# A channel shuffle on one core: other sizes for the first tiles and for the last

## The chip, the core and the metric

The kernel runs on one core of a Trainium2 chip. The metric is device time in microseconds (us) of one execution. The kernel before took 316.17 us (median of three runs, 316.07 to 316.84).

## What is computed

The input is 16 x 64 x 64 pixels with 256 float32 channels each. The channels form 8 groups of 32. The reference turns the (group, channel in group) order of each pixel into (channel in group, group):

```python
x = x.reshape(batch, h, w, groups, channels_per_group)
x = x.transpose(0, 1, 2, 4, 3)
x = x.reshape(batch, h, w, c)
```

No arithmetic is done. Each of the 65,536 pixels is 1 KB; 67.11 MB are read from HBM and 67.11 MB written.

## The kernel before

A tile has 128 partitions, and each partition holds q consecutive pixels, so q KB. In what follows such a tile, or such a part of one, is called "q KB" after its size in one partition; it moves q x 128 KB in all. One kilobyte in all 128 partitions is called a row here: 131,072 bytes. The whole input is 512 rows.

The list `_SLOTS` (L12) says how the 512 rows are cut. Each inner list is one slot: one input tile and one output tile. Each number in it is a part with transfers and a copy of its own. Before, there are two parts of 4 and 8 KB in the first slot, 28 KB in the second, twelve slots of 38 KB, and a last one of 16 KB. All tiles are allocated at the size of the biggest slot (L46, L47). There are two input buffers (L13) and three output buffers (L14), used in turn.

For each slot the loop at L45 does this:

- L55: SyncE's queue (SPq in the profile) issues one read per part, HBM to the input tile. When the slot is at least the third, the issue waits until VectorE has copied out of the input tile two slots earlier.
- L57: VectorE (DVE) copies each part, once its read has landed, from the input tile to the output tile. The permutation is in the access pattern. When the slot is at least the fourth, the copy waits until the output tile three slots earlier has been written to HBM.
- L61: ScalarE's queue (ACTq) issues the write of each part, once its copy is done.

The order on each engine is the order of the program. Reads and writes are thus two queues of transfers, which the page of the profile calls q1 (reads) and q10 (writes), and both are served by the same 16 DMA engines. A read or write of q KB consists of 128 pieces of q KB, one for each partition, and each of the 16 engines moves 8 of them. Each transfer also takes one of eight semaphores in turn; the issue waits until the transfer that had it before has landed.

Of the kernel before, what the change touches and what calls it, by code (L numbers as in the profile page):

```python
# [1 line left out]

# [4 lines left out]


F32 = mybir.dt.float32
P = 128  # L10

_SLOTS = [[4, 8], [28]] + [[38]] * 12 + [[16]]  # L12
_IN_BUFS = 2  # L13
_OUT_BUFS = 3  # L14


@with_exitstack
def kernel(
    ctx: ExitStack,
    tc: tile.TileContext,  # L20
    x: bass.AP,
    groups: bass.AP,
    out: bass.AP,
):
    nc = tc.nc
    b, h, w, c = x.shape
    G = int(groups)
    CPG = c // G
    assert G * CPG == c
    assert sum(map(sum, _SLOTS)) * P == b * h * w  # L30
    biggest = max(map(sum, _SLOTS))

    x_flat = x.rearrange("b h w c -> (b h w c)")
    out_flat = out.rearrange("b h w c -> (b h w c)")

    in_pool = ctx.enter_context(tc.tile_pool(name="in_pool", bufs=_IN_BUFS))
    out_pool = ctx.enter_context(tc.tile_pool(name="out_pool", bufs=_OUT_BUFS))

    def rows(flat, first, q):

        return flat[first * c : (first + P * q) * c].rearrange("(p f) -> p f", p=P)

    ctx.enter_context(tc.manual_schedule(engines=None))
    first = 0
    for parts in _SLOTS:  # L45
        in_tile = in_pool.tile([P, biggest * c], F32, name="in_tile")  # L46
        out_tile = out_pool.tile([P, biggest * c], F32, name="out_tile")  # L47
        at = 0
        pieces = []
        for q in parts:  # L50
            pieces.append((q, first, slice(at * c, (at + q) * c)))
            first += P * q
            at += q
        for q, start, cols in pieces:
            nc.sync.dma_start(out=in_tile[:, cols], in_=rows(x_flat, start, q))  # L55
        for q, start, cols in pieces:
            nc.vector.tensor_copy(  # L57
                out=out_tile[:, cols].rearrange("p (i j g) -> p i j g", j=CPG, g=G),
                in_=in_tile[:, cols].rearrange("p (i g j) -> p i j g", g=G, j=CPG),
            )  # L60
            nc.scalar.dma_start(  # L61
                out=rows(out_flat, start, q), in_=out_tile[:, cols]
            )


# [1 line left out]
_INS = ['x', 'groups']  # L67
_OUTS = [((16, 64, 64, 256), 'float32')]

_NUMBERS = {'groups': 8}  # L70


# [26 lines left out]
```

## Time and profile before

| what | value |
|---|---|
| median of three runs | 316.17 us (316.07 to 316.84) |
| span of the profiled execution, first to last instruction | 314.4 us |
| median time less that span | 1.8 us |
| VectorE busy | 119.0 us, 38% of the span, 16 copies |
| moved by the DMA engines | 134.22 MB, 427 GB/s over the span |
| transfers | 16 reads and 16 writes |

Only the span of the profiled execution is recorded, not its own device time; the timed runs stand 1.8 us above it by their median, for what lies around the first and the last instruction. The profile's page has a row with the busy share of the 16 DMA engines in 40 equal slices of the span (a 9 is 90% or more) and under it the GB/s. A packet in it is one piece of one partition, counted in the slice in which it starts, so that a slice or window can show a share over 1. The trace also holds the start, duration and size of each packet; where a text here says "packet by packet", it is read from there. Times in it count from the first instruction, as in the page.

### The profile page before, as it was taken

To read this page: it belongs to the slowest core of one execution; us is meant where nothing else is said; L and a number is where in the kernel's file an instruction comes from. 1 tells how busy PE (TensorE), PEld (TensorE's weight loads), DVE (VectorE), ACT (ScalarE), POOL (GpSimd) and SP (SyncE) were. 2 spreads that over 40 slices of the span, in tenths; PEclk is the share of its full clock that TensorE was granted. 3 is DMA by queue.
4 is the path that set the end of the run, shared out by engine and by line. 5 is a ranking of instruction groups with operands and counts; after the bars stand their busy time and mean duration, and the time that the engine had idled before them with its cause. 6 is when DMAs were issued, how large, how long until landed. Compare 5 with 4: busy or idle time off the path is not lost.

```text
span 314.4 us, 132 instructions
## 1 busy us (share of the span) xinstructions
DVE 119.0 (38%) x16; POOL 0.2 (0%) x4
## 2 busy tenths in 40 slices
DVE  2081907309109109019028028037046055065400
POOL 0000000000000000000000000000000000000000
DMA  7999999999999999999999999999999999999997
GB/s 317 405 441 416 435 416 483 401 465 406 450 421 446 426 436 436 401 470 396 475 396 475 396 470 401 470 401 470 401 450 421 446 426 436 436 417 450 429 421 321
DMA packets 4608, 134.22 MB, mean 427 GB/s; under 512 B 512, under 2 KB 512, under 8 KB 768
## 3 DMA queue, kind: packets, MB, share of 16 engines
q1 hardware_dynamic: 2304, 67.11, 49.8%
q10 hardware_dynamic: 2304, 67.11, 49.4%
HBM read 67.11 MB, written 67.11 MB: 427 GB/s over the span
## 4 chain that ended last, share of the span: by engine, by line
DMA 76%; DVE 19%; issue 0%; SPq 0%; DVEq 0%
DMA in_tile<-in_x_dram 76%; DVE out_tile L57 19%; SPq L55 0%; DVEq L57 0%
## 5 line engine op out<-in xcount | busy, mean ns | idle before, releaser
L57 DVE COPY out_tile<-in_tile 128x9728 f32<-128x9728 f32 (+4 forms) x16 | 119.0, 7440 | 179.4 <-DMA in_tile<-in_x_dram 179.4
L80 POOL MEMSET const-uint8-127<- 128x1 uint8 x1 | 0.1, 103 | 0.0
L80 POOL MEMSET const-bfloat16-1.0<- 128x1 bf16 x1 | 0.1, 102 | 0.0
L80 POOL MEMSET const-float32-1.0<- 128x1 f32 x1 | 0.1, 100 | 0.0
L80 POOL MEMSET const-float32-0.0<- 128x1 f32 x1 | 0.1, 99 | 0.2 <-issue 0.2
## 6 DMA issues: line engine op xcount, KB each, us to landing
in_tile<-in_x_dram SPq DMA_DIRECT2D x12, 4864.0 KB, 37.0
out_dram<-out_tile ACTq DMA_DIRECT2D x12, 4864.0 KB, 42.6
in_tile<-in_x_dram SPq DMA_DIRECT2D x1, 3584.0 KB, 14.7
out_dram<-out_tile ACTq DMA_DIRECT2D x1, 3584.0 KB, 30.9
in_tile<-in_x_dram SPq DMA_DIRECT2D x1, 2048.0 KB, 30.4
out_dram<-out_tile ACTq DMA_DIRECT2D x1, 2048.0 KB, 15.2
in_tile<-in_x_dram SPq DMA_DIRECT2D x1, 1024.0 KB, 5.4
out_dram<-out_tile ACTq DMA_DIRECT2D x1, 1024.0 KB, 25.0
```

The costliest lines, as they stand in the source:

```text
L57: nc.vector.tensor_copy(out=out_tile[:, cols].rearrange("p (i j g) -> p i j g", j=CPG, g=G), in_=in_tile[:, cols].rearrange("p (i g j) -> ...
L80: nc = _bacc.Bacc("TRN2", target_bir_lowering=False, num_devices=1)
```

## The change

The list of slots is replaced. The first slot has three parts of 4, 6 and 8 KB, the second two of 12 and 16 KB, the third one of 24 KB. Eleven slots of 38 KB follow, one fewer than before, and the last slot has 24 KB in place of 16 KB. The sum is 512 rows as before. There are 15 slots and 18 reads, copies and writes, where there were 15 slots and 16 of each. Buffers, queues and the loop are the same.

```diff
-_SLOTS = [[4, 8], [28]] + [[38]] * 12 + [[16]]
+_SLOTS = [[4, 6, 8], [12, 16], [24]] + [[38]] * 11 + [[24]]
 _IN_BUFS = 2
 _OUT_BUFS = 3
```

## Prediction

> **What bounds the kernel now.** I read the page's rows of slices first, then the table of queues, then the chain, and last the packets one by one.
>
> ```profile
> DVE  2081907309109109019028028037046055065400
> ...
> DMA  7999999999999999999999999999999999999997
> ...
> DMA packets 4608, 134.22 MB, mean 427 GB/s; under 512 B 512, under 2 KB 512, under 8 KB 768
> ...
> q1 hardware_dynamic: 2304, 67.11, 49.8%
> q10 hardware_dynamic: 2304, 67.11, 49.4%
> ```
>
> The DMA row is full in all slices but the first and the last, and the packets of the two queues fill 49.8 + 49.4 = 99.2% of what 16 engines have in the span. VectorE is idle most of the time. So the 16 DMA engines are the bound, and from the first transfer to the last there is no hole in them. The chain of waits could mislead here:
>
> ```profile
> DMA 76%; DVE 19%; issue 0%; SPq 0%; DVEq 0%
> ```
>
> It gives VectorE 19%, as if a shorter copy would shorten the kernel. But the chain follows one thread of work. While VectorE copies, the engines move other tiles: the window from 100 to 150 us, with three copies in it, has a DMA share of 1.01.
>
> ```profile
> 0.00:5.00 5.00, 0.94 (x1) 0.20 (x4) 1.00 0.64 241
> ...
> 100.00:150.00 50.00, 20.66 (x3) 0.00 (x0) 1.00 1.01 436
> ...
> 310.00:315.00 5.00, 0.00 (x0) 0.00 (x0) 1.00 0.53 226
> ```
>
> Packet by packet, the first read starts at 1.75 us and the last write ends at 313.27. The span is thus 1.75 us ahead of the first packet, 311.5 us in which all engines work, and 1.2 us behind the last.
>
> **What the engines' time consists of.** The median durations of a packet are 159 ns for 4 KB, 309 for 8, 611 for 16, 1062 for 28 and 1439 for 38. From 4 to 38 KB that is (1439 - 159) / 34 = 37.6 ns for each KB, and 159 - 4 x 37.6 = 8.4 ns for each packet whatever its size; each transfer ends with one more packet of 9 ns on each engine. One row costs 8 x 37.6 = 301 ns. The 1024 rows of both directions are 308.3 us, the 32 transfers 32 x (8 x 8.4 + 9) ns = 2.4 us. The packets' durations sum to 312.0 us for each engine. The 1.2 us left over are stalls: packets longer than usual for their size. They are nearly all reads, and all but about 0.01 us of them start before 50 us, in stretches in which all 16 engines read at once: 0.54 us in the first 10 us, 0.24 from 10 to 30, 0.36 from 30 to 40.
>
> **The change, part by part.**
>
> *The bytes*: the same 1024 rows, 308.3 us.
>
> *Two more transfers each way*: 4 x (8 x 8.4 + 9) ns = 4 x 76 = **+0.31 us**. Sizes that the trace lacks (6, 12, 24 KB) lie between sizes that it has, all on one straight line within 1 ns, so I see no room in them.
>
> *The first packet and the end*: the first read is 4 KB, as before, so 1.75 us stays. Behind the last write comes the same run of waits and drains, 1.2 us. 0.
>
> *Issues*: SyncE issues two more reads, in about 0.4 us each (the first three start 0.42 and 0.48 us apart), ahead of their need: five reads, 46 rows or 13.9 us of transfer, are asked for by about 2.9 us. The sixth (24 KB) waits for the 8 KB copy. That read is the third, 18 rows, landed by about 8 us; the copy is 2.0 us, so the issue comes at about 10.5 us, when more than 3 us of reads still stand in the queue, even without any write between them. The first 38 KB read waits for the 16 KB copy in the same manner, with the 24 KB read ahead of it. ScalarE's two more issues are off the path. The semaphores that the issues wait for belong to transfers that landed long before: the 24 KB write waits for the 6 KB write, and so on. 0.
>
> *Copies*: four more small copies and one big one less are a few us on an engine that idles for 179.4 us waiting for reads. What hides them is the reads and writes in the queues. 0, as long as the queues hold something, and that has to be checked at the end of the kernel, since the last copy grows: 3.87 us for 16 KB, and for 24 KB, between the rows 3.87 (4096) and 6.57 (7168), 3.87 + 2048 x 2.70 / 3072 = 5.67.
>
> ```profile
> 294.54 3.87 DVE L57 COPY out_tile<-in_tile 128x4096 f32<-128x4096 f32 x1 [7.62 <-DMA in_tile<-in_x_dram]
> ```
>
> **Will the write queue last through the last copy?** When both queues have work, each engine alternates: one read packet, one write packet, whatever their sizes. Near 10 us the 4 KB writes start 1.27 us apart, one 1.06 us read packet between them. That is why small early writes land late:
>
> ```profile
> out_dram<-out_tile ACTq DMA_DIRECT2D x1, 1024.0 KB, 25.0
> ...
> out_dram<-out_tile ACTq DMA_DIRECT2D x1, 512.0 KB, 14.3
> ```
>
> So in 9 turns (8 packets and the closing one) a small write goes out while a large read comes in, and the reads gain a lead. Before: 22 rows are read when the first write starts (9.12 us); the 4 KB write goes out against 5 packets of 28 KB and 3 of 38 KB, 32 rows, lead 50; the 8 KB write against 38 rows, lead 80; the 28 KB write, 90; then 38 against 38 holds it. At the end the 16 KB read comes in against 38 rows of writes: 68. The trace has (313.27 - 292.61) / 0.301 = 69 rows still to write when the last read ends, so the counting works.
>
> After: the first write is issued at the same 5.2 us. Packets taken ahead of it are now of 8 KB, not 28, so it starts about 6.8 us, with 14 rows read. Then 4 KB against 10 rows (half of the 8 and the 12 KB read), lead 20; 6 against 14, 28; 8 against 20, 40; 12 against 31, 59; 16 against 38, 81; 24 against 38, 95. The last read, 24 against 38, leaves **81 rows**.
>
> Needed are the 24 rows of the last tile itself and what covers its copy: 1.9 us from the last read packet to the copy, as before (292.61 to 294.54), 5.67 for the copy and 1.0 from issue to first packet (0.73 to 1.75 at the start), 8.6 us or 29 rows; 53 in all. 81 less 53 leaves 28 rows, 8.4 us of cover. 0.
>
> *The stalls*: here the trace shows no row for the new order. Nearest below is the kernel from 50 us on, where they are nearly nothing, so -1.2 us; nearest above is the same stretch twice over, since mixed sizes now last longer (the lead takes six writes to settle, not three): +1.2 us. I take 0, since the first 10 us, half of it, are much the same, and what else the reads have alone is spread differently but not longer.
>
> Sum: **+0.3 us**, with -0.9 and +1.5 as ends. On the profiled execution that is 314.4 + 0.3 = 314.7; the median of the runs stands 1.8 above its span, so 316.17 + 0.3 = **316.5 us**. About 0.3%, 0.95 us, is what a measurement of this kernel tells from no change: the line to faster is 315.2, to slower 317.1.
>
> **Rivals.**
>
> *Stalls grow (slower).* Their place is the first 60 us, while reads get more of the engines than writes. For it: 5.7 of the 19 engine-us of stalls fall at 32 to 34 us, when the engines each take two 38 KB reads in a row. Against it: the new sizes rise more gently, so fewer such pairs. Twice the stalls give 316.5 + 1.2 = 317.7; it decides for slower from 0.65 us more than now (0.95 less 0.31).
>
> *Stalls vanish (faster).* 316.5 - 1.2 = 315.3. For it: from 50 us on there are none. Against it: 0.54 us come in the first 10 us, when only reads can run. Even in full this hardly passes the line.
>
> *The write queue runs dry at the end (slower).* It decides if the lead at the last read is under 53 rows. If the lead stayed at the 40 rows of the 8 KB write, 14 fewer at the end, 27 rows would be missing: 27 x 0.301 = 8.1 us, 324.6. That takes engines that share by bytes and not by packets, which the 1.27 us between the small writes and the 69 rows speak against.
>
> *Each further transfer pays a fixed time (slower).* The 512 KB read takes 3.3 us from issue to landing, its packets 1.9 us (1.75 to 3.67); 1.4 us are fixed. If four more transfers paid that unhidden: 5.6 us, 322.1. Against it: 32 transfers would then have left 45 us of holes, and there are 2.9 us outside the packets. The Trainium skill ("DMA: Bandwidth & Descriptors", "Anatomy of one DMA") fits a DMA as about 2.0 us plus its bytes over 436 GB/s, for transfers issued from GpSimd; an estimate by that, four times 2.0 us, would be 8 us more. The trace does not agree for a filled queue: its share is 99.2%.
>
> **How the numbers follow.** The forecast, within 0.3%: 0.68. Stalls grow: 0.14, of which 0.11 pass the line. Stalls vanish: 0.11, of which 0.06 pass it (with the runs' own spread, 0.77 us). Dry queue: 0.04. Fixed time: 0.03. So faster 0.06, same 0.68 + 0.05 + 0.03 = 0.76, slower 0.11 + 0.04 + 0.03 = 0.18. The range takes in the ends of the stalls, 315.3 to 317.7, and leaves out the last two rivals and what passes the ends.
>
> **What would show it.** Right: a DMA row of 9s from the second slice to the last but one, queue shares that sum to about 99%, writes of the first parts that land sooner than 14.3 and 25.0 us, and some 20 us or more from the last copy's start to the end of the span (19.9 before; 81 rows are 24 us of writes from the last read packet, less 1.9, plus 1.2). Wrong: a slice under 9 inside, above all behind the last read; GB/s under 400 over more than one early slice; a copy that waits for a write.

## The result, and the profile after

The changed kernel is slower: 318.4 us as the ratio to the kernel before gives it, 1.0071 with an interval of 1.0049 to 1.0093. The median of its four runs was 318.81 us, beside 316.12 for the kernel before. One of the four took 342.88 us, far from the other three (317.75 to 319.17), and the ratio leaves it out, as the ratios below leave out one run of e1_head (342.25 us) and two of e4_slotwrite (331.15 and 332.01 us). The forecast was 316.5, with 315.3 to 317.7 as its range.

The page of the changed kernel, in the rows that were read before: VectorE and the DMA engines in 40 slices, the GB/s, the packets, the two queues, and the chain.

```profile
DVE  3452528073460550650740830820910901907000
...
DMA  8999999989999999999999999999999999999994
GB/s 308 399 434 473 392 436 418 476 385 432 446 462 403 462 403 462 398 467 398 467 398 467 393 472 403 462 408 457 428 437 428 433 442 422 426 444 433 433 434 214
DMA packets 5184, 134.22 MB, mean 424 GB/s; under 512 B 576, under 2 KB 576, under 8 KB 1088
...
q1 hardware_dynamic: 2592, 67.11, 49.5%
q10 hardware_dynamic: 2592, 67.11, 49.2%
...
another core or an unknown queue 38%; DVE 29%; DMA 23%; SPq 0%; issue 0%; DVEq 0%
```

The ninth slice shows an 8. That is no hole: a packet counts in the slice in which it starts, and by the packets' starts and ends all 16 engines are busy throughout that slice. What differs is the last slice: 4 in place of 7, 214 GB/s in place of 321. Something works there, but not all of it. The end in windows shows it better. The columns are the stretch, its length, VectorE, GpSimd, the granted clock, the mean share of the 16 DMA engines and the GB/s. First the kernel before, then the changed one:

```profile
312.00:313.00 1.00, 0.00 (x0) 0.00 (x0) 1.00 0.65 279
313.00:314.00 1.00, 0.00 (x0) 0.00 (x0) 1.00 0.00 0
```

```profile
312.00:313.00 1.00, 0.00 (x0) 0.00 (x0) 1.00 0.91 393
313.00:314.00 1.00, 0.00 (x0) 0.00 (x0) 1.00 0.12 49
314.00:315.00 1.00, 0.00 (x0) 0.00 (x0) 1.00 0.11 49
```

A share of 0.12 is 2 / 16: two DMA engines work alone for about 2 us while fourteen have finished. The packets say the same. The trace doesn't name the engine of a packet, but each transfer ends with one closing packet on each of the 16 engines, so these 16 times show how far the engines are apart. For the last write, their median is 312.92 us before and 313.13 after, 0.22 later. The latest engine is 0.37 us behind that median before, and 2.21 after; the second latest 1.87. So of the 2.2 us between the two profiled spans (314.44 and 316.66), 0.22 is on all engines, 2.21 - 0.37 = 1.84 is two engines that are late, and 0.17 lies behind the last packet.

The packets also show where the two lose their time. On one engine each packet starts some nanoseconds before the one ahead of it ends, so from 60 us on they can be linked into 16 chains, one for each engine. In the changed kernel 14 packets are over 0.05 us longer than usual for their size. All of them lie on the two chains that end late, 1.94 and 1.87 us in sum, and none on the other fourteen.

The row of the chain (the last one in the first fence above) now puts the most time down to a name that is no engine, and the waits say what VectorE waits for:

```profile
DVE out_tile L57 <- DMA out_dram<-out_tile: 142.6, 11, 14.3
DVE out_tile L57 <- DMA in_tile<-in_x_dram: 28.1, 7, 9.4
```

Before, all 179.4 us of its waiting was for reads. Now eleven copies wait until an output tile has been written: the reads' lead has grown until all three output tiles are in use. That is the most visible difference between the two profiles, and the experiments had to find out whether it is the one that costs.

### The profile page after: what moved, and what is told of

The parts are those of the page before. It is cut to its first block, busy times and chain, and to the rows that moved or that the text cites. A ratio compares the mean times of both kernels' runs of the same rounds, so it can differ in the third digit from the quotient of the medians.

```text
span 316.7 us, 143 instructions
## 1 busy us (share of the span) xinstructions
DVE 120.6 (38%) x18; POOL 0.2 (0%) x4
## 4 chain that ended last, share of the span: by engine, by line
another core or an unknown queue 38%; DVE 29%; DMA 23%; SPq 0%; issue 0%; DVEq 0%
DVE out_tile L57 29%; DMA out_dram<-out_tile 15%; DMA in_tile<-in_x_dram 8%; SPq L55 0%; DVEq L57 0%
## 5 line engine op out<-in xcount | busy, mean ns | idle before, releaser
L57 DVE COPY out_tile<-in_tile 128x9728 f32<-128x9728 f32 (+6 forms) x18 | 120.6, 6698 | 170.7 <-DMA out_dram<-out_tile 142.6
```

Of the source, the lines that this page charges most:

```text
L57: nc.vector.tensor_copy(out=out_tile[:, cols].rearrange("p (i j g) -> p i j g", j=CPG, g=G), in_=in_tile[:, cols].rearrange("p (i g j) -> ...
```

## Which part of the change, and which wait

Three readings were open: A, the waiting for output tiles costs; B, the bigger last tile does; C, the many mixed sizes do by themselves.

**The new head alone (e1_head).** The third slot has 32 KB, so that the sum stays 512 rows with the old end.

```diff
-_SLOTS = [[4, 8], [28]] + [[38]] * 12 + [[16]]
+_SLOTS = [[4, 6, 8], [12, 16], [32]] + [[38]] * 11 + [[16]]
```

> The new head with the old end: slots of 4+6+8, 12+16, 32, eleven of 38 and 16 KB, 18 transfers each way less none, so the two further ones of the changed kernel are in it. The changed kernel is 2.2 us above the one before (ratio 1.0071); in its trace two of the 16 DMA engines end 2 us after the other fourteen, and from the sixth 38 KB copy on the copies wait for output tiles to be written. Theory A (the reads' lead over the writes grows to the three output tiles, and in that state single engines fall behind): the lead comes from the head, so 318 us or more, two or more engines late, copies that wait for writes. Rival B (the bigger last tile leaves engines unevenly finished): 316.5 us, engines within 0.5 us of each other. Rival C (many mixed sizes throw engines out of step, whatever the lead): 318 us or more as with A.

Measured: 1.0146 times the kernel before (1.0124 to 1.0169). Copies wait 144.5 us for output tiles. In its profile four engines end 1.60 to 3.18 us behind the median:

```profile
313.00:314.00 1.00, 0.00 (x0) 0.00 (x0) 1.00 0.27 115
314.00:315.00 1.00, 0.00 (x0) 0.00 (x0) 1.00 0.15 66
315.00:316.00 1.00, 0.00 (x0) 0.00 (x0) 1.00 0.08 33
```

The shares fall step by step as one engine after the other finishes: about 4 of 16, then 2, then 1. The new head alone thus brings a loss, twice that of the changed kernel.

**The new end alone (e2_tail).** Here the second slot has 20 KB in place of 28, for the same reason.

```diff
+_SLOTS = [[4, 8], [20]] + [[38]] * 12 + [[24]]
```

> The old head, with 20 in place of 28 KB, and the new end: slots of 4+8, 20, twelve of 38 and 24 KB; 16 transfers each way. Theory A: the lead is settled by the 4 and 8 KB writes as before, a little higher for the 20 KB write (18 against 10 rows), about 98 rows, so it stays under the 114 of three output tiles: 316.2 us, within 0.5 us, copies that wait for reads. Rival B (the end): 318 us or more with engines late by 2 us. Rival C (mixed sizes at the head): 316.2 us.

Measured: 1.0008 (0.9999 to 1.0017). B falls: with 24 KB at the end the time is the same within 0.17%, 0.5 us, as the prediction's cover for the last copy said.

**The kernel before, with 4+4+4 KB first (e3_pinned).**

```diff
+_SLOTS = [[4, 4, 4], [28]] + [[38]] * 12 + [[16]]
```

> The kernel before with its first slot cut in 4+4+4 KB in place of 4+8, nothing else: one more transfer each way, 0.15 us. The third 4 KB write goes out against 38 KB reads, so by the counting of turns the lead rises by some 30 rows, from 90 to over 114, and copies have to wait for output tiles. Theory A: about 318 us, one or more engines 1 us or more late, copies that wait for writes. Rivals B and C (the end is the old one, and the sizes at the head are fewer than in the changed kernel): 316.3 us, within 0.5 us.

Measured: 1.0075 (1.0062 to 1.0088), copies waiting 152.3 us for output tiles, two engines 2.55 and 2.69 us late. So one small part more is enough for the whole loss, which speaks against C, and A looked right.

**The changed kernel with one write for each slot (e4_slotwrite).** The reads and copies are those of the changed kernel; the first three writes have 18, 28 and 24 KB.

```diff
+        nc.scalar.dma_start(
+            out=rows(out_flat, first, total), in_=out_tile[:, : total * c]
+        )
```

> The changed kernel's slots and reads, with one write for each slot (18, 28, 24 KB, then 38) in place of one for each part; 18 reads, 15 writes. Writes of 18 and 28 KB hold the lead down: by the counting of turns it settles near 80 to 95 rows, under three output tiles. Theory A: 316.3 us, within 0.5 us, engines together at the end, copies that wait for reads. Rival B (the end): 318 us or more. Rival C (mixed sizes): 318 us, or something between, since the read sizes are the changed kernel's.

Measured: 1.0026 (1.0016 to 1.0035), 0.8 us, copies that wait for reads, engines within 0.7 us of each other at the end. Again as A says. But A had so far been tested only by kernels whose small first parts changed too.

**The kernel before with two output buffers (e5_before_two_out).** This makes copies wait for output tiles and changes nothing else. The closing packets gave a second theory beside A, D: some engines fall out of step. In the changed kernel two engines, and in e1_head four, close the third write (8 KB) 1.0 to 1.3 us ahead of the median and stay apart from then on; in the kernel before none does.

```diff
-_OUT_BUFS = 3
+_OUT_BUFS = 2
```

> The kernel before with two output buffers in place of three, nothing else. Its lead of about 90 rows then stands over the 76 rows of two output tiles, so copies wait for output tiles, with the old sizes at the head. The runs so far leave two theories. A (waiting for output tiles is what costs): 318 us or more. D (the first writes come in while the engines move small read packets; some engines take their first write one turn ahead of the others or behind them, stay out of step, and meet longer packets): in the kernel before all 16 engines take the first write in the same turn, so 316.3 us within 0.5 us, and the engines end within 0.5 us of each other although copies wait for writes.

Measured: 1.0000 (0.9990 to 1.0011). Its waits and its DMA row:

```profile
DVE out_tile L57 <- DMA out_dram<-out_tile: 168.1, 13, 14.2
DVE out_tile L57 <- DMA in_tile<-in_x_dram: 13.2, 3, 7.6
```

```profile
DMA  8999999999999999999999999999999999999997
```

VectorE waits even longer for writes here than in the changed kernel, and it costs nothing: the DMA row is full in every slice inside. **A falls**, as far as it is the waiting. All 16 engines are in step (within 0.42 us at the last closing packet). The reads' lead itself is not tested by this run: by the closing packets 64 rows are left to write when the reads end, as in the kernel before, where the changed kernel has 110.

**32 KB slots, with four and with three output buffers (e6_32_four_out, e7_32_three_out).**

```diff
+_SLOTS = [[4, 6, 8], [12, 16], [24]] + [[32]] * 13 + [[26]]
+_OUT_BUFS = 4
```

> The changed kernel's head (4+6+8, 12+16, 24), then thirteen slots of 32 KB and 26 KB last, with four output buffers of 32 KB (128 rows): 20 transfers each way, 0.3 us more than the changed kernel's 18 in packets and closing packets. By the counting of turns from a first write at 9.4 us the lead settles near 108 rows, under four output tiles, so copies wait for reads. A: 316.9 us, within 0.5 us. D: engines out of step as in the changed kernel, 318 us or more, whatever the output buffers.

> The same sizes with three output buffers (96 rows): copies wait for output tiles. A: 318.5 us or more, and more than with four. D: the same time as with four output buffers, 318 us or more.

Measured: 1.0102 (1.0077 to 1.0127) with four buffers, where all copies wait for reads, and 1.0063 (1.0043 to 1.0083) with three, where copies wait 146.1 us for writes. It is slower either way. More telling are the single runs. With four buffers they lie between 316.30 and 321.02 us, with three between 316.33 and 318.71. The profiled run of each is its fastest, and in both no engine is out of step. A fixed cost of these sizes, C, cannot give that: the same program runs at the kernel before's time in one run and 2 to 5 us slower in the next.

## When an engine out of step costs

**No small head at all (e8_plain).**

```diff
+_SLOTS = [[38]] * 13 + [[18]]
```

> No small head at all: thirteen slots of 38 KB and one of 18, 14 transfers each way, two fewer than the kernel before: -0.3 us of packets. The first write comes at about 23 us, while the engines move 38 KB packets; two reads of 38 rows, 23 us of transfer, stand ahead of the third, which waits for the first copy, so the read queue just lasts. A and D both: engines in step, lead about 76 rows, copies that wait for reads: 315.9 us, with more read stalls in the first 23 us (all engines read alone) up to 317. If the DMA row shows a hole near 23 us, the read queue ran dry.

Measured: 1.0498 (1.0478 to 1.0519). Both theories missed. The read queue does run dry near 25 us, 0.6 us of all engines; reads and writes then start together, and the read packets of that moment take 0.5 to 2.0 us longer, 1.4 us of all engines. The rest is a standing loss, seen in the two queues, which before had almost equal shares:

```profile
q10 hardware_dynamic: 2016, 67.11, 50.8%
q1 hardware_dynamic: 2016, 67.11, 47.9%
```

Two engines are out of step, ahead of the other fourteen by 1.2 us more with each tile. This time the two keep nearly all their packets at 1.44 us, and it is the writes of the fourteen that are long: 1.60 us in the mean from 60 to 245 us. Eight packets of 0.16 us more make 1.3 us a tile. So here the long packets lie on the majority, and the two that are out of step have almost none.

**28 KB as one part, in the changed kernel (e9_28), and cut in the kernel before (e10_cut28).**

```diff
+_SLOTS = [[4, 6, 8], [28], [24]] + [[38]] * 11 + [[24]]
```

```diff
+_SLOTS = [[4, 8], [12, 16]] + [[38]] * 12 + [[16]]
```

> The changed kernel with 28 KB as one part in place of 12+16 in its second slot, nothing else: 17 transfers each way. The first write, issued at 5.2 us and started near 9.4, then comes in while the engines move 28 KB read packets of 1.06 us, several times the 0.3 to 0.6 us by which the engines are apart, in place of 12 KB ones of 0.46 us. Theory D: all 16 engines take it in the same turn, stay in step, 316.4 us within 0.5 us, in most runs, although the lead stands at three output tiles and the other mixed sizes are there. Rival C (the mix of sizes, 4, 6, 8, 24 and 24, or the further transfers): 317.5 us or more.

> The kernel before with 12+16 KB in its second slot in place of 28, nothing else: 17 transfers each way, +0.15 us. The first write now comes in among 12 KB packets. Theory D: some engines take it a turn apart, 317.3 us or more in most runs, times that spread over 1 us or more, and the engines out of step at the end by 1 us or more where the profiled run is one of those. Rival C: two sizes more and one transfer more: 316.3 us, within 0.5 us.

Measured: 1.0016 (1.0008 to 1.0025) and 1.0015 (1.0007 to 1.0024). The first time is what D expected, but not for D's reason: three engines are out of step in that profile. Nor is the lead at three output tiles, as was expected: all its copies wait for reads. The second is a miss: two engines are out of step, as expected, and the median run costs 0.34 us, 0.15 of it for one more transfer each way. So being out of step is not yet the cause.

**12 KB as one first part (e11_one_head).**

```diff
+_SLOTS = [[12], [28]] + [[38]] * 12 + [[16]]
```

> The kernel before with 12 KB as one part in place of 4+8 in its first slot: 15 transfers each way, -0.15 us. The first write is issued near 9 us and starts near 13, among 28 KB packets, or at their end among 38 KB ones. Theory D: in step, 316.0 us within 0.4 us. Rival C: the same. It is the candidate to beat the kernel before, by what one transfer less each way is worth; and if engines fall out of step here, small packets are not the only way to it.

Measured: 1.0025 (1.0014 to 1.0036), slower, a miss too. Reads are stalled for 0.73 us, taken over all engines, between 10 and 15 us, when the first write comes in; the kernel before has 0.06 there.

**The changed kernel once more (e12_after_again).**

> The changed kernel once more, beside these. Theory D: whether and how many engines fall out of step is not the same in each run, so 316.4 us in a run in which none does, 317.5 to 319.5 in the others, a spread over 1 us, where the kernel before spreads by some tenths. Rival C (a fixed cost of the sizes): all runs within 0.5 us of each other, near 318.4.

Measured: 1.0054 (1.0031 to 1.0077), twelve runs from 316.50 to 320.96 us, four of them at 316.50 to 316.57. The spread is what D said. (It is not the changed kernel's alone: the kernel before took 317.41 us in one of its runs, e5_before_two_out 317.69, and e10_cut28 317.99.) The profiled run is the one of 316.50, and four engines are out of step in it, more than in the first profile. Its end:

```profile
312.00:313.00 1.00, 0.00 (x0) 0.00 (x0) 1.00 0.91 393
313.00:314.00 1.00, 0.00 (x0) 0.00 (x0) 1.00 0.01 0
```

All 16 engines finish together, so **D falls as it stood**. What differs is by how much they are out of step. By 100 us the four are 1.37 to 1.45 us behind in reads and 1.34 to 1.42 ahead in writes: about one packet of 38 KB, 1.44 us. Their reads lie on the others' writes, edge on edge, and from 100 to 260 us no packet is longer for it. At the end of the reads the lag turns back into nothing, since each engine has the same bytes to move. In the first profile the two were 1.83 and 2.13 us behind. Their packets lay across the others' turns, and one write or read a tile took 0.1 to 0.45 us longer (1.57 to 1.88 us in place of 1.44), at about 102, 125, 149 and 172 us. They dropped back until they were 3.3 and 3.6 us behind in reads, somewhat over one whole turn of a read and a write (2.88 us).

**Further profiles (s1_after, s2_after, s4_head, s6_32_four_out).** The first two are the changed kernel, then the program of e1_head, then that of e6_32_four_out. They were taken to tell two theories apart. S says that an engine out of step costs nothing while its lag is about one packet, and ends late when the lag is larger; its range for one packet of 38 KB, 1.3 to 1.55 us, was drawn from the profiles so far. T says that only the number of such engines counts.

> The changed kernel, for a further profile. S: each engine that is out of step with an offset of 1.3 to 1.55 us near 120 us ends with the others (within 0.5 us); one with 1.57 to 2.9 us ends 1 us or more late, and the time is 316.5 us if there is none of these, 317.5 or more if there is. T: the more engines are out of step, the longer, whatever their offset.

> The changed kernel, for a further profile: as for the one before it.

> The new head with the old end, whose first profile had four engines at offsets of 1.57 to 1.68 us near 105 us, all late at the end by 1.6 to 3.2 us. S: the same where offsets are off 1.3 to 1.55, 316.6 us where they are in it. T: by the number of engines.

> The new head with 32 KB slots and four output buffers, whose profile had no engine out of step (316.3 us) while other runs took 318 to 321 us. One packet of 32 KB is 1.21 us. S: engines out of step at an offset within 0.15 us of 1.21 cost nothing, others end 1 us or more late. T: by the number of engines. With none out of step, 316.3 us, and nothing is told apart.

The table has all profiles with engines of this kind, by the closing packets. The lag in reads is against the median of 16, for the read that closes next after 100 us (for s6_32_four_out the read near 92 us, where a packet has 32 KB and 1.21 us; at its next read, at 111 us, the lag is 1.80); lateness is that at the last write.

| run | us | engines out of step: lag in reads, us | late at the end, us |
|---|---|---|---|
| e12_after_again | 316.50 | 1.37, 1.38, 1.42, 1.45 | none over 0.3 |
| s1_after | 316.39 | 1.37 | none over 0.3 |
| e9_28 | 316.43 | 1.30, 1.49, 1.54 | none over 0.3 |
| e10_cut28 | 316.48 | 1.26, 1.30 | none over 0.3 |
| the changed kernel | 318.44 | 1.83, 2.13 | 1.87, 2.21 |
| s2_after | 318.36 | 1.66, 1.68, 1.91 | 1.69, 2.13, 2.16 |
| e1_head | 319.37 | 1.57, 1.61, 1.62, 1.68 | 1.60, 1.76, 1.96, 3.18 |
| s4_head | 318.88 | 1.59, 1.64, 1.67, 1.81 | three by 1.85 to 2.64; the one at 1.59 not |
| s6_32_four_out | 318.56 | 1.38 | 2.42 |

The four new profiles came out as S says, but for the engine at 1.59, which stands at the edge and lost nothing until the end. T falls: a single engine costs 2.4 us in s6_32_four_out, and four cost nothing in e12_after_again. The end in windows of s1_after and then of s2_after, the same program in two runs:

```profile
313.00:314.00 1.00, 0.00 (x0) 0.00 (x0) 1.00 0.01 0
```

```profile
313.00:314.00 1.00, 0.00 (x0) 0.00 (x0) 1.00 0.18 74
314.00:315.00 1.00, 0.00 (x0) 0.00 (x0) 1.00 0.11 49
```

Besides e8_plain, three profiles have engines out of step in another way and don't fit the table: e2_tail one engine (0.81 us ahead in reads, 2.04 behind in writes) that ends 0.60 late without any longer packets, e11_one_head two (0.8 to 0.9 us ahead in reads, 1.7 to 1.8 behind in writes) that end 0.5 late, and e3_pinned two (1.1 to 1.3 us behind in reads from 131 us, and 4.0 in writes).

**What stays open.** No run shows why a packet that lies across the others' turns is longer, why the fourteen have the long packets in e8_plain and the few elsewhere, or what sets the lag. Four engines of e12_after_again were 0.49 to 0.53 us behind at 60 us and came to one packet, three of s2_after were 0.55 to 0.75 behind and came to 1.66 and more. One part can be read off: each of the three in s2_after has a read of 1.70 to 1.77 us at 65 us, each of the two in the first profile one of 1.83 or 1.87, and in e12_after_again none is over 1.50. Less these excesses, the lag grows by 0.83 to 0.86 us an engine from 60 to 100 us in all three profiles. So in these profiles a long read is part of what takes the lag past one packet, and no run shows why it comes in one run and not in another. S rests on profiles of runs as they fell; no kernel here sets the lag on purpose. Nor need a profile stand for the usual run: in e1_head, e4_slotwrite, e6_32_four_out, e7_32_three_out, e8_plain, e9_28 and e12_after_again the profiled run is the fastest.

One rival was left untested, the size of the reads' lead. By the closing packets, the five kernels with a median over 317.5 us (the changed one, e1_head, e3_pinned, e6_32_four_out and e7_32_three_out) have 92 to 110 rows left to write when the reads end; the other kernels have 50 to 86, and all of these but e8_plain stay at 317.1 us or below in their median. The lead alone doesn't set the time, since e12_after_again and s1_after took 316.50 and 316.39 us with 110 rows. Whether a large lead is what lets engines get late, no run shows.

## Why the prediction was wrong, point by point

- **The bound** was read rightly. By the packets' starts and ends the DMA engines are busy in every slice inside, before and after. Two signs that the prediction took for wrong came all the same without a hole behind them: the 8 of the ninth slice, and GB/s under 400 in the second, fifth and ninth (399, 392, 385). Packets counted where they start give both. Three signs that it took for right came too: the queues' shares sum to 98.7%, the writes of 4, 6 and 8 KB land in 9.7, 14.8 and 22.4 us, and 31 us pass from the start of the last copy to the end. None of these five looks at the engines one by one.
- **Two more transfers, 0.31 us**: right. The packets' durations sum to 312.50 us for each engine in the mean, 0.50 more, of which 0.31 is this and 0.20 stalls; the closing packet of the median engine comes 0.22 us later. The two profiled runs of the changed kernel in which no engine is late took 316.39 and 316.50 us, and three more runs 316.52 to 316.57: the forecast of 316.5 is what a run takes when no engine is late. It is not the usual run: eight of the twelve in e12_after_again took 317.19 us or more.
- **The stalls**: this is the step that failed. It took the stalls as one sum divided by 16, and their ends as that sum gone or doubled. The sum hardly moved, from 1.16 to 1.36 us. But the kernel ends with its slowest engine, and the stalls after 60 us, 3.8 us of one engine's time, fell on two engines, 1.9 us on each. The kernel paid 1.84 us where the mean shows 0.2. Each engine has its own eight pieces of every transfer, and what the two had lost was not evened out by the end. The forecast of 316.5 and these 1.84 us make the 318.3 that the measured 318.4 stands at; why the packets of the two engines were long stays open.
- **The rival "stalls grow"** had the sign. Its place was wrong, since the first 60 us are much as before (1.15 us of stalls before, 1.12 after) and the long packets of the two engines come between 65 and 245 us. Its mechanism, all engines reading at once, is not the one either: reads and writes alternate there, and the long packets are of both kinds.
- **The lead** was mis-sized. The first write was to start at about 6.8 us; it started at 9.40, hardly other than before (9.12), although the reads ahead of it were smaller. So the lead passed three output tiles, and copies waited for writes: the sign that the prediction named as wrong. At the end some 110 rows were left ((313.1 - 280.0) / 0.301, by the closing packets of the median engine; 64 before by the same count), not 81. e5_before_two_out shows that the waiting by itself costs nothing; it does not show that of the lead.
- **The cover of the last copy**: right. e2_tail has the bigger last tile at no cost, and the last slices stay full until the two late engines.
- **A dry write queue, a fixed time for each transfer**: neither came. The runs of e6_32_four_out and e7_32_three_out with all engines in step have 20 transfers each way and take 316.3 us, 0.2 more than the kernel before with its 16. The estimate that the prediction made by the Trainium skill ("DMA: Bandwidth & Descriptors", "Anatomy of one DMA"), 2.0 us for each transfer, is thus not what these queues show.

## What to carry to other kernels

Where a row of the profile is a mean over parallel units, ask what the slowest unit does: a mean that is nearly unchanged can hide a tail, and the last slice of the DMA row shows it (a share of 2 / 16 is two engines). Where both queues are always full, other sizes of the first tiles have little to win: here no list of sizes ran faster than the kernel before, one transfer more each way cost 0.15 us in packets, and several lists lost 2 us or more to engines that ended late. Time such a change in many runs and look at the spread: 316.4 and 319 us from one program say more than their median.

## What the runs showed of the hardware

- Each DMA engine alternates between a read packet and a write packet, whatever their sizes, and the closing packet takes a turn of its own. The Trainium skill ("DMA: Bandwidth & Descriptors", "Queues, rings and completion order") has the engines go round the queues packet by packet, and gives 9 to 17 descriptors (single moves) as typical for a packet. The traces agree on the going round, not on the size: what takes turns here is one partition's piece, 4 to 38 KB. This order is stable: engines one packet apart near 100 us are still one packet apart at 260 us (e12_after_again, s1_after).
- A packet that lies across the others' turns took up to 1.88 us in place of 1.44 in the first profile of the changed kernel. In e8_plain, with two engines out of step, the writes of the fourteen others took 1.60 us in the mean, and the kernel 16 us longer; no run shows how the one makes the other.
- From the issue of the first write to its first packet 3.9 us pass before (5.19 to 9.12) and 4.0 after (5.36 to 9.40), with reads in the queue, where the first read takes 1.0 (0.73 to 1.75).
